# Float16 parts for the input projection's last eight tiles, in a one-core encoder layer

## The chip, the cores and the metric

The kernel runs on one core of a Trainium2 chip. The metric is the device time of one launch in microseconds; lower is better. A core has five engines that work beside each other, each in its own listed order: TensorE (PE, matmuls; PEld is its weight load), VectorE (DVE), ScalarE (ACT), GpSimd (POOL) and SyncE (SP), on whose queue most DMA transfers are issued.

## The reference

One encoder layer on 1024 tokens of width 1024: a normed input, one projection to 2304 columns, two token mixers on its parts, an output projection, and a gated MLP with a depthwise convolution.

```python
hn = rmsnorm(h, norm_mix[l])
proj = jnp.einsum('bsd,de->bse', hn, w_in[l])
qa, ka, va, qb, kb, vb = jnp.split(proj, splits, axis=-1)
...
o_a = window_gqa_sink(qa, ka, va, sink[l])                # |i-j| <= 128, 8 heads
o_b = neighbourhood_attention(qb, kb, vb, rpb[l])         # 8 x 16 window on a 16 x 64 grid, 8 heads
mix = jnp.concatenate([rmsnorm(o_a, norm_a[l]), rmsnorm(o_b, norm_b[l])], axis=-1)
h = h + jnp.einsum('bse,ed->bsd', mix, w_out[l])
hn = rmsnorm(h, norm_ffn[l])
h = h + conv_gated_mlp(hn, w_gate[l], w_up[l], conv_w[l], conv_b[l], w_down[l])
return rmsnorm(h, norm_final)
```

All values are float32.

## The kernel before

Activations lie transposed, with features on the 128 partitions and tokens along the free axis. A float32 product is made of three matmuls on a high and a low part of each operand: high by high, high by low, low by high. `block` issues these three for one 128 by 128 weight block and 512 tokens (half `h` of the 1024). In the input projection the parts are of the type float32r (rows of the profile call it f32); in the output projection (`product16`, L180) and the MLP (L1197 to L1199) they are float16, with scales found on the chip.

The input projection has 18 tiles of 128 columns. `Project(m)` makes tile `m`: 8 blocks (`k`, 128 features each) for each half, 16 blocks or 48 matmuls. Its right operands are `xg[k]`, the high and low part of x times the norm gain, 16 tiles of 512 KB under the tag "xg". Its weights come in two loads (`load`, `load_rest`), each of 4 blocks: `fetch_w` loads a raw tile, `halve_w` (L156, L157) makes `whi` on ScalarE and `wlo` on VectorE or, from unit 12 of the attention on, on POOL. `evacuate` (L269, L273) multiplies the result by `rstd1`, the row factors of the norm, and `post` turns it into attention operands.

Tiles 0 to 2 are made ahead. The others, then the first half of the output projection (`OutA`), form a list `jobs` that is run by a generator, `rest`, as filler between the attention's steps: the loop over `units` (16 units of the window, 32 of the grid) issues scores, transposes and value products, and calls `fill` after each, at the rates in `RATES`. That fixes TensorE's order by hand. The other engines' order comes from a scheduler, which follows the order of writing, priorities and its own estimates. The dictionary `aux` holds extra steps by (number of the job, number of its block); the job of tile `m` has the number `m - 3`.

A score row goes through VectorE (L466, with the mask or bias), ScalarE (exponential, L470), VectorE (reciprocal, L471), and then reaches the value product by one of several paths: scaled on POOL (L474) and transposed on TensorE (L498), then split by ScalarE and VectorE (L501, L502); or split first (L480, L481, L484 to L491) and transposed by a DMA on SP's queue ("flip", L492). `split_v` (L353 on) scales and splits values with ScalarE (L375) and VectorE (L376).

Before the attention, `scan_out` loads the 8 tiles of the output weights once and sums their squares on ScalarE (L761); from these `out_scales`, an `aux` step at (8, 3), finds the scale `wo_by` of the output weights' float16 parts, with two transposes on TensorE (L255).

Of the kernel before, what the change touches and what calls it, by code (L numbers as in the profile page):

```python
# [13 lines left out]
F32 = mybir.dt.float32  # L14
# [42 lines left out]
V_TOP, P_TOP, TINY = 2.0 ** 14, 2.0 ** 15, 1e-30  # L57
X_TOP, W_TOP, FAINT = 2.0 ** 7, 2.0 ** 13, 1e-24
W_ROOT = W_TOP * 2.0 ** 63

K_ID, K_MA, K_MB, K_SCALE, K_END = 0, 128, 512, 896, 897


def hybrid_layer(tc, xT, w_in, w_out, w_gate, w_up, w_down, small, sink, rpb, consts, rope, out):
    nc = tc.nc
    with ExitStack() as ctx:
# [92 lines left out]

        def load_w(src):  # L160
            return halve_w(fetch_w(src))

        def load_w16(src):

# [188 lines left out]
        def split_v(t, rows):  # L353

            n = rows.stop - rows.start
            top, down = (vpool.tile([128, 1], F32, name=x, tag=x) for x in ("top", "down"))
            up = cpool.tile([128, 1], F32, name="up", tag="up", bufs=6)
            nc.vector.tensor_reduce(top[rows], t[rows, :], axis=mybir.AxisListType.X, op=ALU.max, apply_absolute_value=True)
            nc.vector.tensor_scalar(top[rows], top[rows], TINY, None, op0=ALU.max)
# [267 lines left out]
        class Project:  # L627
            def __init__(self, m):
                self.m, self.grid = m, m >= 6

            def load(self):
                raw, self.raw = (fetch_w(w_in[self.m, :, k:k + 4, :]) for k in (0, 4))
                self.w = halve_w(raw)

            def load_rest(self):
                self.w += halve_w(self.raw)

            def run(self):
                self.t = tmp("t")
                if self.m < 17:  # L640
                    for h in range(2):
                        ps = bank("pj", "pj")
                        yield from product(ps, self.w, xg, h)
                        with tc.high_priority(offset=500), behind(*["low"] * (self.m == 3 and h == 1)):
                            evacuate(self.t, ps, h, self.grid)
                else:

                    ps = [bank("pj", "pj") for _ in range(2)]
                    for h, k in [(h, i - 3 * h) for i in range(KT + 3) for h in range(2) if 0 <= i - 3 * h < KT]:
                        block(ps[h], self.w[k], xg[k], h, k == 0, k == KT - 1)  # L650
# [104 lines left out]
        wo_rows = cpool.tile([128, KT], F32, name="wo_rows")  # L755
        mix_up, wo_by, wo_back = (cpool.tile([128, 1], F32, name=x) for x in ("mix_up", "wo_by", "wo_back"))

        def scan_out(d):
            t = big("scan", "op")
            nc.sync.dma_start(t, w_out[d].rearrange("p k c -> p (k c)"))  # L760
            nc.scalar.activation(t, t, AF.Square, accum_out=wo_rows[:, d:d + 1])  # L761
# [68 lines left out]
        def rest():  # L830
            for i, job in enumerate(jobs[1:]):
# [3 lines left out]
                for n, _ in enumerate(job.run()):  # L835
                    yield True
                    if i == 0:
                        if n == 8:
                            with behind("copied"):
                                for p in first:  # L840
                                    make_stacks(p)
                        continue
                    if n == REST and i + 2 < len(jobs):
                        jobs[i + 2].load_rest()
                    settle(n)
                    if (i, n) in aux:
                        aux[i, n]()
# [38 lines left out]
        aux[11, 8] = square_a  # L886
        for h in range(2):
            aux[12, 10 + 3 * h], aux[13, 1 + 2 * h] = (lambda h=h: narrow_a(h)), (lambda h=h: wide_a(h))
        for i in range(4):
            aux[13, 3 * i + 4], aux[13, 3 * i + 6] = normed_a(i, 0), normed_a(i, 1)  # L890
        def out_scales():

            m = top(par[:, C_NA:C_NA + 8], "pt", "og")
# [14 lines left out]
        SCAN_OUT_AT, OUT_SCALES_AT = [], (8, 3)  # L908
        for d, x in enumerate(SCAN_OUT_AT):
            aux[x] = lambda d=d: scan_out(d)  # L910
        aux[OUT_SCALES_AT] = out_scales
        aux[13, 3] = lambda: (wide_a(1), gains_up(0))
        filler = rest()
        live["op"] = 2 + sum(needs(m) for m in range(3))

# [993 lines left out]
```

## Time and profile before

| | |
|---|---|
| median of 3 runs | 1028.36 us (1027.37 to 1029.76) |
| profiled execution | 1028.71 us, span 1026.6 us |
| busy over the span | PE 1009.0, PEld 577.2, DVE 875.2, ACT 675.8, POOL 214.6 us |
| granted clock of TensorE | 0.997 |
| input projection with attention | to about 301 us |
| output projection | to about 410 us |

A row of a group gives the line, the engine, the operation, output and inputs, their shape and type, the count, then busy time and the mean of one in ns, then the idle time before it and what ended it. In rows in order of time the first two numbers are start and duration in us.

### The profile page before, as it was taken

To read this page: it belongs to the slowest core of one execution; us is meant where nothing else is said; L and a number is where in the kernel's file an instruction comes from. 1 tells how busy PE (TensorE), PEld (TensorE's weight loads), DVE (VectorE), ACT (ScalarE), POOL (GpSimd) and SP (SyncE) were. 2 spreads that over 40 slices of the span, in tenths; PEclk is the share of its full clock that TensorE was granted. 3 is DMA by queue.
4 is the path that set the end of the run, shared out by engine and by line. 5 is a ranking of instruction groups with operands and counts; after the bars stand their busy time and mean duration, and the time that the engine had idled before them with its cause. 6 is when DMAs were issued, how large, how long until landed. Compare 5 with 4: busy or idle time off the path is not lost.

```text
span 1026.6 us, 15663 instructions
## 1 busy us (share of the span) xinstructions
PE 1009.0 (98%) x5102; PEld 577.2 (56%) x5102; DVE 875.2 (85%) x1715; ACT 675.8 (66%) x1242; POOL 214.6 (21%) x339
## 2 busy tenths in 40 slices
PE   8999999999999999999999999999999999999996
PEld 6877777777775555544444444444444444444446
DVE  6799997767898799999897989888888879999865
ACT  7667787768687687645777777844544656655551
POOL 2225545777976210001000000000000000000002
PEclk9999999999999999999999999999999999999998
DMA  8566564786799874201787777723232778978734
GB/s 318 194 134 134 111 141 102 154 160 134 141 190 226 287 254 165 82 1 42 258 279 248 262 242 250 246 99 128 87 122 89 256 250 306 309 242 269 257 141 164
DMA packets 143938, 191.79 MB, mean 187 GB/s; under 512 B 77360, under 2 KB 88112, under 8 KB 143856
## 3 DMA queue, kind: packets, MB, share of 16 engines
q1 hardware_dynamic: 133264, 164.84, 56.2%
q10 hardware_dynamic: 10592, 25.95, 6.6%
q8 instruction: 40, 0.66, 0.3%
q14 instruction: 42, 0.34, 0.1%
HBM read 132.81 MB, written 28.57 MB: 157 GB/s over the span
## 4 chain that ended last, share of the span: by engine, by line
PE 75%; DVE 3%; DMA 2%; ACT 1%; issue 0%; POOL 0%; DVEq 0%; ACTq 0%; POOLq 0%
PE pj L180 7%; PE dn L1199 6%; PE dn L1198 6%; PE dn L1197 6%; PE z L1197 5%; PE z L1198 5%; PE z L1199 5%; PE x L1197 4%; PE y L1197 4%; PE x L1198 4%; PE y L1198 4%; PE y L1199 4%; PE x L1199 4%; PE pj L172 3%; PE pj L174 2%; PE pj L173 2%
## 5 line engine op out<-in xcount | busy, mean ns | idle before, releaser
L1199 PEld LDWEIGHTS <-wlo 128*128 128x128 f16 x898 | 87.9, 98 | 101.3
L1197 PEld LDWEIGHTS <-whi 128*128 128x128 f16 x898 | 88.1, 98 | 100.3
L1198 PEld LDWEIGHTS <-whi 128*128 128x128 f16 x898 | 87.9, 98 | 100.2
L1199 PE MATMUL dn<-xd,wlo 128*128 128x512 f16 (+1 forms) x330 | 120.4, 365 | 0.0
L1198 PE MATMUL dn<-xd,whi 128*128 128x512 f16 (+1 forms) x330 | 120.4, 365 | 0.0
L1197 PE MATMUL dn<-xd,whi 128*128 128x512 f16 (+1 forms) x330 | 120.4, 365 | 0.0
L172 PE MATMUL pj<-xgh,whi 128*128 128x512 f32 x248 | 106.8, 431 | 0.0
L1197 PE MATMUL z<-hg,whi 128*128 128x512 f16 x264 | 100.1, 379 | 0.0
L1198 PE MATMUL z<-hg,whi 128*128 128x512 f16 x264 | 100.1, 379 | 0.0
L1199 PE MATMUL z<-hg,wlo 128*128 128x512 f16 x264 | 100.1, 379 | 0.0
L470 ACT ACTIVATE p<-p,nm 128x385 f32<-128x385 f32 (+3 forms) x128 | 74.8, 584 | 35.7 <-DVE nm L466 27.1
L174 PE MATMUL pj<-xgh,wlo 128*128 128x512 f32 x248 | 97.7, 394 | 0.0
L173 PE MATMUL pj<-xgl,whi 128*128 128x512 f32 x248 | 97.4, 393 | 0.0
L1171 ACT ACTIVATE whi<-ws,m 128x512 f16<-128x512 f32 (+1 forms) x96 | 65.9, 708 | 35.6 <-DVE ws L1338 20.4
L1172 DVE SCALAR_TENSOR_TENSOR wlo<-ws,m,whi 128x512 f16<-128x512 f32 (+1 forms) x96 | 70.2, 741 | 17.9 <-ACT whi L1171 17.7
L1052 POOL TENSOR_TENSOR back<-back,cst 128x4 f32<-128x4 f32 (+1 forms) x7 | 2.8, 394 | 356.7 <-DVE back L1051 356.7
L1186 ACT ACTIVATE scan<-scan 128x1024 f32<-128x1024 f32 (+1 forms) x60 | 61.1, 1018 | 18.0 <-DMA scan<-in_w_down_dram 13.6
L1171 ACT ACTIVATE whi<-raw,m 128x512 f16<-128x512 f32 (+1 forms) x78 | 51.3, 699 | 17.7 <-DMA raw<-in_w_down_dram 9.6
L1172 DVE SCALAR_TENSOR_TENSOR wlo<-raw,m,whi 128x512 f16<-128x512 f32 (+1 forms) x78 | 55.4, 731 | 6.9 <-ACT whi L1171 6.9
L1197 PE MATMUL y<-hg,whi 128*128 128x512 f16 x160 | 60.6, 379 | 0.0
L1198 PE MATMUL y<-hg,whi 128*128 128x512 f16 x160 | 60.6, 379 | 0.0
L1199 PE MATMUL y<-hg,wlo 128*128 128x512 f16 x160 | 60.6, 379 | 0.0
(299 smaller groups left out, 2457.7 us busy)
## 6 DMA issues: line engine op xcount, KB each, us to landing
xd<-x SPq DMA_DIRECT2D x77, 256.0 KB, 5.5
raw<-in_w_down_dram SPq DMA_DIRECT2D x64, 256.0 KB, 3.6
x<-c ACTq DMA_DIRECT2D x22, 512.0 KB, 3.7
scan<-in_w_gate_dram SPq DMA_DIRECT2D x18, 512.0 KB, 4.5
scan<-in_w_up_dram SPq DMA_DIRECT2D x18, 512.0 KB, 6.1
raw<-in_w_gate_dram SPq DMA_DIRECT2D x18, 512.0 KB, 3.9
raw<-in_w_up_dram SPq DMA_DIRECT2D x18, 512.0 KB, 3.5
raw<-in_w_in_dram SPq DMA_DIRECT2D x32, 256.0 KB, 3.1
```

Of the source, the lines that this page charges most:

```text
L172: nc.tensor.matmul(ps, w[0], x[0][:, tsl(h)], start=first, stop=False)
L173: nc.tensor.matmul(ps, w[0], x[1][:, tsl(h)], start=False, stop=False)
L174: nc.tensor.matmul(ps, w[1], x[0][:, tsl(h)], start=False, stop=last)
L180: nc.tensor.matmul(ps, a, b, start=i == 0 and b is x[h][0] and a is w[0], stop=i == len(ws) - 1 and a is w[1])
L470: nc.scalar.activation(p[:, 0:e], p[:, 0:e], AF.Exp, bias=nm, scale=-1.0, accum_out=sm)
L1052: nc.gpsimd.tensor_tensor(back, back, unit_back.to_broadcast([128, n]), op=ALU.mult)
L1171: mark["whi"] = nc.scalar.activation(hi, src, AF.Copy, scale=by)
L1172: nc.vector.scalar_tensor_tensor(lo, src, by, hi, op0=ALU.mult, op1=ALU.subtract)
L1186: nc.scalar.activation(t, t, AF.Square, accum_out=dst)
L1197: nc.tensor.matmul(ps, w[0], x[0], start=first and i == 0, stop=False, skip_group_check=True)
L1198: nc.tensor.matmul(ps, w[0], x[1], start=False, stop=False, skip_group_check=True)
L1199: nc.tensor.matmul(ps, w[1], x[0], start=False, stop=last and i == len(ws) - 1, skip_group_check=True)
```

## The change

Tiles 10 to 17 of the input projection take float16 parts instead of float32r: tiles 10 and 11 for the blocks k = 0 to 3 (their blocks k = 4 to 7 stay float32r, with weights scaled alike), tiles 12 to 17 for all. For this

- `scan_in` takes the place of `scan_out` at the start: it loads the weight tiles 10 to 17 and sums their squares on ScalarE;
- `in_tops` and `in_scales`, during tile 8, find scales for x and the weights from the gains, the smallest row factor and these sums: three reductions and some column operations on VectorE, two transposes on TensorE, three operations on POOL;
- `x_fetch` loads the 8 tiles of x a second time, four during tile 9 and four during tile 11, into places of the tag "xg"; `x_halve` makes the float16 parts from them, the high one on ScalarE, the low one on VectorE;
- `halve_w16` and `halve_scaled` first scale the raw weights in place on ScalarE, then split them on ScalarE and POOL;
- `rstd1` is multiplied on ScalarE, at the start of tile 10, by the inverse of the scales;
- tiles 9 to 12 are made in another order, four blocks for each half, then the other four for each half, tiles 10 and 11 with k = 4 to 7 first, in two banks of PSUM at a time;
- the scans of the output weights (`fetch_out`, `scan_out`) are spread over tiles 12 to 14, and `out_scales` moves to tile 15.

```diff
+G_MIN, Y_TOP = 2.0 ** -40, 2.0 ** 9
+HALF_AT = (10, 12)
+M_END = 18
...
+        def halve_w16(raw):
+            hi, lo = (wpool.tile([128, 4, 128], F16, name=n, tag=n, padded_shape=[128, 8, 128]) for n in ("whi", "wlo"))
+            nc.scalar.activation(raw, raw, AF.Copy, scale=wi_by)
+            nc.scalar.activation(hi, raw, AF.Copy)
+            nc.gpsimd.tensor_tensor(lo, raw, hi, op=ALU.subtract)
...
+            def halve(self, i, raw):
+                how = halve_w if self.m < HALF_AT[0] else halve_w16 if self.m >= HALF_AT[i] else halve_scaled
...
+                self.turned = HALF_AT[0] <= self.m < HALF_AT[1]
+                order = (1, 0) if self.turned else (0, 1)
...
+                x = [x16[k] if self.m >= HALF_AT[k // 4] else xg[k] for k in range(KT)]
+                if HALF_AT[0] - 1 <= self.m <= HALF_AT[1]:
+                    ps = [bank("pj", "pj") for _ in range(2)]
+                    for i in (1, 0) if self.turned else (0, 1):
+                        for h in range(2):
+                            for k in range(4 * i, 4 * i + 4):
+                                block(ps[h], self.w[k], x[k], h, k % 4 == 0 and (i == 1) == self.turned, k % 4 == 3 and (i == 0) == self.turned)
+                                yield
...
+        def fetch_out(d):
+            wo_scan[d] = big("scan", "xg")
+            nc.sync.dma_start(wo_scan[d], w_out[d].rearrange("p k c -> p (k c)"))
         def scan_out(d):
-            t = big("scan", "op")
-            nc.sync.dma_start(t, w_out[d].rearrange("p k c -> p (k c)"))
+            t = wo_scan.pop(d)
             nc.scalar.activation(t, t, AF.Square, accum_out=wo_rows[:, d:d + 1])
...
+        def in_tops():
+            for i, rows in enumerate((par[:, C_NMIX:C_NMIX + 8], wi_rows)):
+                nc.vector.tensor_reduce(wi_top[:, i:i + 1], rows, axis=mybir.AxisListType.X, op=ALU.max, apply_absolute_value=True)
+            nc.vector.tensor_reduce(x_least, rstd1, axis=mybir.AxisListType.X, op=ALU.min)
...
+        def x_fetch(k):
+            x_again[k] = big("xt", "xg")
+            nc.sync.dma_start(x_again[k], xT[k])
+        def x_halve(k):
+            t = big("x16", "xg").bitcast(F16)
+            hi, lo = x16[k] = t[:, 0:S], t[:, S:2 * S]
+            by = x_gains[:, k:k + 1]
+            nc.scalar.activation(hi, x_again[k], AF.Copy, scale=by)
+            nc.vector.scalar_tensor_tensor(lo, x_again[k], by, hi, op0=ALU.mult, op1=ALU.subtract)
...
-        for d in range(KT):
-            scan_out(d)
+        for m in range(HALF_AT[0], M_END):
+            scan_in(m)
...
+        at(HALF_AT[0] - 5, 3, in_tops)
+        at(HALF_AT[0] - 5, 8, in_scales)
+        at(HALF_AT[0] - 3, 1, lambda: nc.scalar.activation(rstd1, rstd1, AF.Copy, scale=wi_back))
+        for i, m in enumerate((HALF_AT[0] - 1, HALF_AT[1] - 1)):
+            for k in range(4):
+                at(m - 3, 5 + k, lambda k=4 * i + k: x_fetch(k))
+                at(m - 3, 8 + 2 * k, lambda k=4 * i + k: x_halve(k))
...
-        aux[OUT_SCALES_AT] = out_scales
+        for d in range(KT):
+            at(9 + d // 3, 2 + 5 * (d % 3), lambda d=d: fetch_out(d))
+            at(9 + (d + 1) // 3, (7, 12, 2)[d % 3], lambda d=d: scan_out(d))
+        at(12, 6, out_scales)
```

Lines in the rows below are those of each program: L191 to L193 of the new one are L172 to L174 of the old (`block`), L456 is L436 (scores), L490 is L470 (exponential), L512 is L492 (flip).

TensorE at the 79th score row, before:

```order
1209 L172 MATMUL pj<-xgh,whi 128x512
1210 L173 MATMUL pj<-xgl,whi 128x512
1211 L174 MATMUL pj<-xgh,wlo 128x512
1212 L436 MATMUL s<-ka,q 128x384
1213 L436 MATMUL s<-kb,q 128x384
```

and the same place now, where `x_2719` is the pair of float16 parts of x's tile k = 4:

```order
1280 L191 LDWEIGHTS whi
1281 L191 MATMUL pj<-x_2719,whi 128x512
1282 L192 LDWEIGHTS whi
1283 L192 MATMUL pj<-x_2719,whi 128x512
1284 L193 LDWEIGHTS wlo
1285 L193 MATMUL pj<-x_2719,wlo 128x512
1286 L456 MATMUL s<-ka,q 128x384
1287 L456 MATMUL s<-kb,q 128x384
```

The number and order of the matmuls is the same; the float16 ones have a weight load listed apart, and use float16 tiles.

ScalarE during tile 9, from the 47th exponential of the attention on, before:

```order
184 L470 ACTIVATE p,sm<-p,nm 128x385
185 L501 ACTIVATE turned<-pt 128x3x128
186 L485 ACTIVATE stage<-p,by 128x3x128
187 L470 ACTIVATE p,sm<-p,nm 128x385
188 L480 ACTIVATE hl<-p 128x3x128
189 L501 ACTIVATE turned<-pt 128x3x128
190 L470 ACTIVATE p,sm<-p,nm 128x385 x2
```

and now, with L851 for the high half of one tile of x (`x_2149` and so on) from the reloaded `xt`, and L170 for a half of the weights:

```order
191 L505 ACTIVATE stage<-p,by 128x3x128
192 L851 ACTIVATE x_2149<-xt,cells 128x1024
193 L490 ACTIVATE p,sm<-p,nm 128x385
194 L170 ACTIVATE whi<-raw 128x512
195 L490 ACTIVATE p,sm<-p,nm 128x385
196 L521 ACTIVATE turned<-pt 128x3x128
197 L851 ACTIVATE x_2172<-xt,cells 128x1024
198 L500 ACTIVATE hl<-p 128x3x128
199 L490 ACTIVATE p,sm<-p,nm 128x385
200 L556 ACTIVATE ot<-o 64x256
201 L851 ACTIVATE x_2225<-xt,cells 128x1024
202 L851 ACTIVATE x_2256<-xt,cells 128x1024
```

Four halvings, each behind a load of 512 KB, have come between the exponentials.

SP's queue at that place, before:

```order
78 L492 DMA_TRANSPOSE turned<-stage 128x6x128
79 L150 DMA raw<-in_w_in_dram 128x512
80 L492 DMA_TRANSPOSE turned<-hl 128x6x128
81 L492 DMA_TRANSPOSE turned<-stage 128x6x128 x2
82 L492 DMA_TRANSPOSE turned<-hl 128x6x128
83 L150 DMA raw<-in_w_in_dram 128x512
```

and now, with L844 for `x_fetch`:

```order
81 L512 DMA_TRANSPOSE turned<-stage 128x6x128
82 L844 DMA xt<-in_xT_dram 128x1024 x3
83 L512 DMA_TRANSPOSE turned<-stage 128x6x128
84 L844 DMA xt<-in_xT_dram 128x1024
85 L153 DMA raw<-in_w_in_dram 128x512
86 L512 DMA_TRANSPOSE turned<-hl 128x6x128
87 L844 DMA xt<-in_xT_dram 128x1024 x3
88 L512 DMA_TRANSPOSE turned<-stage 128x6x128 x2
```

Seven of the eight loads of x now stand within seven rows, between the flips, and behind one another.

More of the change, by code (lines that the diff above doesn't have):

```diff
@@ L161, in load_w, with halve_scaled @@
             return halve_w(fetch_w(src))
+        def halve_w16(raw):
[3 more added lines that the diff above has]
+            nc.gpsimd.tensor_tensor(lo, raw, hi, op=ALU.subtract)
+            return [(hi[:, j, :], lo[:, j, :]) for j in range(4)]
+        def halve_scaled(raw):
+            hi, lo = (wpool.tile([128, 4, 128], F32R, name=n, tag=n) for n in ("whi", "wlo"))
+            nc.scalar.activation(raw, raw, AF.Copy, scale=wx_by)
+            nc.scalar.activation(hi, raw, AF.Copy)
+            nc.gpsimd.tensor_tensor(lo, raw, f32(hi[:, :, :]), op=ALU.subtract)
+            return [(hi[:, j, :], lo[:, j, :]) for j in range(4)]
         def load_w16(src):
@@ L355, in split_v @@
             n = rows.stop - rows.start
-            top, down = (vpool.tile([128, 1], F32, name=x, tag=x) for x in ("top", "down"))
+            topdown = vpool.tile([128, 2], F32, name="top", tag="top")
+            top, down = topdown[:, 0:1], topdown[:, 1:2]
             up = cpool.tile([128, 1], F32, name="up", tag="up", bufs=6)
@@ L845, in rest @@
                     settle(n)
-                    if (i, n) in aux:
-                        aux[i, n]()
+                    for f in aux.get((i, n), ()):
+                        f()
                 if i == 0:
```

60 lines of the change are left out of this document (46 added, 14 removed).

## The prediction

> **What bounds the kernel now.** I read the page's shares and chain first, then the groups by line, the stretches of the attention, the waits of TensorE, and last single matmuls in order of time.
>
> ```profile
> PE 1009.0 (98%) x5102; PEld 577.2 (56%) x5102; DVE 875.2 (85%) x1715; ACT 675.8 (66%) x1242; POOL 214.6 (21%) x339
> PE 75%; DVE 3%; DMA 2%; ACT 1%; issue 0%; POOL 0%; DVEq 0%; ACTq 0%; POOLq 0%
> ...
> L172 PE MATMUL pj<-xgh,whi 128*128 128x512 f32 x248 | 106.8, 431 | 0.0
> L1197 PE MATMUL z<-hg,whi 128*128 128x512 f16 x264 | 100.1, 379 | 0.0
> ```
>
> TensorE (PE) is busy for 98% of the span and carries the chain of waits. The durations in a matmul's row include its way through the array, so 431 and 379 ns are no prices: what one costs is the step from its start to the next start. The change concerns projection tiles 10 to 17, and those fall between about 170 and 301 us (the evacuations of L273, two a tile from tile 6 on, run from 98.5 to 301.2 us). How full are the engines there, and does TensorE ever stop?
>
> ```profile
> 130.00:150.00 20.00, 19.04 (x107) 14.31 (x106) 17.87 (x54) 16.16 (x42) 10.29 (x23) 1.00 0.76 156
> 150.00:170.00 20.00, 20.00 (x117) 15.32 (x115) 15.92 (x50) 15.09 (x39) 9.67 (x21) 1.00 0.33 73
> 170.00:190.00 20.00, 19.56 (x116) 14.94 (x115) 16.73 (x60) 15.86 (x43) 12.11 (x20) 1.00 0.68 137
> 190.00:205.00 15.00, 14.79 (x82) 11.38 (x81) 9.50 (x38) 9.54 (x25) 12.91 (x18) 1.00 0.82 173
> 205.00:255.00 50.00, 50.00 (x275) 39.22 (x274) 34.66 (x103) 35.85 (x80) 36.72 (x44) 1.00 0.76 148
> 255.00:301.00 46.00, 46.00 (x260) 36.18 (x259) 40.91 (x106) 34.18 (x73) 38.81 (x43) 1.00 0.83 158
> ...
> L273 DVE TENSOR_TENSOR t<-pj,rstd x24: 669/682/692, 98.5 to 301.2; 128x512 f32<-128x512 f32 x24
> ...
> PE o L525 <- DVE by L484: 1.4, 1, 1.4
> PE pt L498 <- POOL p L474: 1.4, 3, 0.7
> PE pj L180 <- DVE mg L1144: 1.2, 1, 1.2
> ```
>
> The columns of the stretches are length, then PE, PEld, DVE, ACT, POOL busy, the granted clock (1.00 throughout) and DMA share. From 150 to 301 us TensorE is busy 150.35 of 151 us while no other engine is full. The three waits shown are its longest from 60 to 420 us and sum to 4.0 us. So in the stretch of the change its own instructions set the time, and what shortens them shortens the span, as long as nothing else fills up.
>
> **The change, part by part. 1. Cheaper matmuls.** A block is three matmuls of 512 columns. Tiles 10 and 11 move 8 of their 16 blocks to float16, tiles 12 to 17 all 16: 112 blocks, 336 matmuls. Float32 blocks with nothing between, and float32 and float16 blocks amid attention, stand in order of time:
>
> ```profile
> 21.83 0.39 PE L172 MATMUL o<-xgh,whi 128*128 128x512 f32 x1
> ...
> 23.89 0.39 PE L172 MATMUL pj<-xgh,whi 128*128 128x512 f32 x1
> ...
> 201.07 0.40 PE L172 MATMUL pj<-xgh,whi 128*128 128x512 f32 x1
> ...
> 203.21 0.40 PE L172 MATMUL pj<-xgh,whi 128*128 128x512 f32 x1
> ...
> 203.92 0.50 PE L601 MATMUL o<-turned,v 128*128 128x128 f16 x4
> ...
> 310.23 0.60 PE L180 MATMUL pj<-mg,whi 128*128 128x512 f16 x2
> ...
> 310.88 0.49 PE L601 MATMUL o<-turned,v 128*128 128x256 f16 x4
> ...
> 312.22 0.60 PE L180 MATMUL pj<-mg,whi 128*128 128x512 f16 x2
> ```
>
> Nine float32 matmuls from 21.83 to 23.89 are 0.229 us each, 0.687 a block. Amid attention one block, 203.21 to 203.92, is 0.71; a float16 one, 310.23 to 310.88, is 0.65. The whole pattern of block, four value matmuls, block, two scores takes 2.14 us (201.07 to 203.21) in float32 and 1.99 (310.23 to 312.22) in float16: 0.075 a block. So the ends are 112 x (0.687 - 0.65) = 4.1 us and 112 x 0.075 = 8.4; I take the single-block rows, nearest in kind and place, 112 x 0.06 = **6.7 us less**. Float16 matmuls have a separate weight load in the instruction list where float32 ones have none, but the trace's float16 blocks have that too, so 0.65 includes it.
>
> The Trainium skill speaks against this gain: "TensorE: Matmul & The Clock Gate", section "Back-to-back issue gap", gives one warm gap, N/2.4 + 2.5 ns, with no word of the type, so 216 ns for 512 columns in either. By it this term would be 0, and the sum below would be 3.4 us slower instead of 3.3 faster. The trace has 0.217 for float16 (0.65 by three) but 0.229 to 0.237 for float32, so the formula holds for the one and not for the other.
>
> **2. ScalarE (ACT).** Added work, by the nearest rows:
>
> ```profile
> L375 ACT ACTIVATE vhl<-t,down 128x1024 f16<-128x1024 f32 x4 | 4.5, 1136 | 0.0
> L167 ACT ACTIVATE whi<-raw,wo_by 128x512 f16<-128x512 f32 x8 | 5.7, 711 | 0.9 <-PE pj L180 0.9
> L761 ACT ACTIVATE scan<-scan 128x1024 f32<-128x1024 f32 x8 | 8.4, 1056 | 0.0
> L761 ACT ACTIVATION_READ_ACCUMULATOR scan<-scan 128x1 f32 x8 | 1.6, 196 | 0.0
> ...
> 26.97 1.05 ACT L761 ACTIVATE scan<-scan 128x1024 f32<-128x1024 f32 x1
> ...
> 28.00 1.06 ACT L761 ACTIVATE scan<-scan 128x1024 f32<-128x1024 f32 x1
> ```
>
> Eight high halves of x at 1.14 us are 9.1; sixteen scalings of half a weight tile in place at 0.71 are 11.4; eight out-weight scans, formerly before the attention, at 1.25 are 10.0 (the input-weight scans take their old place one for one, at no cost); the scaling of the row factors 1.1. That is 31.6 us. By place: 150 to 190 us gets four halves of x, four scalings and the row factors, 8.5, on 30.95 of 40; 190 to 205 four halves and two scalings, 6.0, on 9.54 of 15; 205 to 255 the scans and six scalings, 14.3, on 35.85 of 50. So ScalarE's busy time comes to 39.5 of 40, 15.5 of 15 and 50.2 of 50. Busy time overstates it: a scan's two rows sum to 1.25, but the next scan starts 1.03 after it (26.97 to 28.00), so about 0.1 us an instruction overlaps. With 187 instructions there before and 37 more, up to 22 of the 105 us are overlap, though part of it shows as no busy time already; I put real use near 90 to 95%. What does such a load do to TensorE? Slices of before that are as full:
>
> ```profile
> 240.00:250.00 10.00, 10.00 (x58) 7.87 (x57) 6.27 (x19) 8.29 (x19) 5.57 (x9) 1.00 0.76 161
> 290.00:300.00 10.00, 10.00 (x58) 7.86 (x58) 9.29 (x22) 9.15 (x17) 7.25 (x7) 1.00 0.93 190
> 300.00:310.00 10.00, 9.35 (x57) 5.80 (x56) 9.01 (x29) 8.88 (x21) 6.88 (x9) 1.00 1.18 250
> 360.00:370.00 10.00, 8.82 (x43) 4.16 (x42) 10.00 (x21) 9.74 (x19) 0.00 (x0) 1.00 0.75 294
> ...
> 360.00:410.00 50.00, 48.82 (x265) 26.89 (x264) 47.26 (x85) 39.73 (x70) 4.27 (x7) 1.00 0.60 210
> ```
>
> With ACT at 8 to 9 tenths TensorE lost nothing or 0.65; at 9.74 beside a full DVE it lost 1.18. Ends for 105 us: 0, since nothing is taken from ScalarE that could give a gain, and 10.5 x 1.18 less the 0.65 that TensorE idles there already (19.56 of 20, 14.79 of 15), some 11.7. I take 2.5, a quarter of a microsecond a slice, near the fuller slices of the attention itself (0 and 0.65), since scores run ahead of the values that use them.
>
> **3. VectorE (DVE), POOL, TensorE's new steps.** Eight low halves of x at 1.31 (row below) are 10.5 us: 5.2 in 150 to 170, on 15.92 of 20, so over it in busy time and carried into 170 to 190; 5.2 in 190 to 205, where 5.5 are free. The reduction over the row factors (1.21) lands early, after the first tiles' evacuations near 46 us, where VectorE works without a break. I price what of both shows on TensorE at 0.6, between 0 and 1.21 + 1.2 (one carry as large as the excess of 21.1 over 20). POOL keeps its subtractions and gains a few column operations of 0.25 to 0.6 us: no cost, since the scores' scaling waits for VectorE there. Two transposes (0.27 each) and the scan's move past OUT_SCALES add 0.3 on TensorE.
>
> ```profile
> L376 DVE SCALAR_TENSOR_TENSOR vhl<-t,down,vhl 128x1024 f16<-128x1024 f32 x4 | 5.2, 1310 | 0.0
> L358 DVE TENSOR_REDUCE top<-t 128x1 f32<-128x1024 f32 x4 | 4.8, 1210 | 0.0
> ...
> xt<-in_xT_dram SPq DMA_DIRECT2D x6, 512.0 KB, 6.1
> xr<-in_xT_dram SPq DMA_DIRECT2D x6, 512.0 KB, 4.6
> scan<-in_w_out_dram SPq DMA_DIRECT2D x8, 512.0 KB, 8.4
> q1 hardware_dynamic: 133264, 164.84, 56.2%
> ```
>
> **4. Transfers.** Sixteen loads of 512 KB move into 150 to 255 us on SP's queue, among the flips (DMA transposes of the probabilities). The main queue's 164.84 MB took 56.2% of the span, 577 us, so 8.4 MB take 29 of 105 us and raise a DMA share of 0.33 to 0.82 by 0.28. Alone that is hidden, as 205 to 255 us ran at 0.76 with TensorE at 50.00. Their latency is not free: the first x loads wait until TensorE has used the float32 tiles they overwrite, and ScalarE's four halvings stand within four exponentials of each other (its order, in the section on the change). That is in the 2.5 above, and beyond it a rival.
>
> Sum: -6.7 + 2.5 + 0.6 + 0.3 = **-3.3 us**. The profiled execution took 1028.71 us (span 1026.6), 0.35 above the median of 1028.36; from the latter, **1025.1 us**.
>
> **The rivals.** (a) The covers hold: 2 and 3 cost nothing but the transposes, 1028.4 - 6.7 + 0.3 = 1022.0. For it: scores run ahead by two or three units, and the waits of 4.0 us in 360. Against: the sums at 15.5 of 15. (b) ScalarE and VectorE fill up and pace the attention: 5 to 6 us given back, about 1028. For it: the same sums, and VectorE at 40.91 of 46 behind. (c) Slower: ScalarE held by loads. It works in its listed order; if an x tile or a scan lands late, every exponential behind it waits, then POOL's scaling, then the transposes, which already wait thrice for POOL above. A load in a queue took 8.4 us where 4.6 is the free time, so up to 3.8 late; a set of four x tiles holds that once, and two sets and two bursts of scans make 4 x 3.8 = 15 on ScalarE, of which it decides when more than 6.7 - 3.4 = 3.3 reach TensorE. With half through, 1028.4 - 3.3 + 7 = 1032. (d) No gain by type: 1028.4 + 3.4 = 1031.8; for it only that 0.229 lies near 0.217, against it the float16 pattern at 1.99. It is what the Trainium skill's gap formula, above, would give.
>
> **How the numbers follow.** Forecast 0.43 (own range 1023.4 to 1026.2); (a) 0.17; (b) 0.25; (c) 0.12; (d) 0.03. A measurement here tells 0.2%, 2.06 us, from no change. Faster: 0.43 + 0.17 = 0.60; same: (b) 0.25; slower: 0.15. The range leaves out (c), (d) and the outer part of (a), and reaches through (b): 1021.7 to 1029.6.
>
> **What would show it.** Right: float16 blocks of pj at 0.65 us a block; the last evacuation of tile 17 some 3 us before 301.2; the FFN stages as long as before; ScalarE above 90% from 150 to 255 us, with TensorE's busy time there short by 2 to 4 us. Wrong: blocks still at 0.70; waits of ScalarE for xt or scan over a microsecond each, with pt or o waiting behind (c); or TensorE without gaps (a). A gain that appears by 301 us and is gone by 410 would mean that the next stage was paced by VectorE (47.26 of 50 in 360 to 410), which I leave at nothing since its work follows TensorE's results.

## The result, and the profile after

The changed kernel took 1054.2 us (median of 6 runs, 1052.07 to 1058.1) against 1028.72 for the kernel before (6 runs): a ratio of 1.0253, 95% interval 1.0238 to 1.0269. It is 25.5 us slower; 3.3 us faster had been forecast. The profiled execution has a span of 1050.7 us (1026.6 before). Two executions further below ran at a granted clock of 0.65 (1497 and 1499 us) and are left out of the ratios, and since the only profile of the kernel with the high half first is of one of them, its waits are not read. The lines that answer to those shown of before, from the page, the stretches, the evacuations and TensorE's waits from 60 to 440 us:

```profile
PE 1012.7 (96%) x5104; PEld 555.0 (53%) x5104; DVE 886.9 (84%) x1734; ACT 702.6 (67%) x1283; POOL 220.5 (21%) x343
PE 62%; DVE 4%; DMA 3%; ACT 2%; issue 1%; SPq 0%; POOL 0%; DVEq 0%; ACTq 0%; POOLq 0%
```

```profile
130.00:150.00 20.00, 19.05 (x107) 14.25 (x106) 17.03 (x58) 15.82 (x40) 11.58 (x25) 1.00 0.67 148
150.00:170.00 20.00, 18.45 (x103) 13.48 (x101) 17.64 (x46) 17.97 (x39) 10.98 (x20) 1.00 0.63 173
170.00:190.00 20.00, 16.01 (x85) 10.82 (x83) 16.43 (x53) 16.09 (x40) 10.96 (x17) 0.91 0.86 225
190.00:205.00 15.00, 14.98 (x85) 10.39 (x84) 12.36 (x35) 12.76 (x30) 12.02 (x14) 1.00 0.59 99
205.00:255.00 50.00, 44.51 (x253) 25.50 (x251) 29.70 (x91) 40.37 (x89) 31.10 (x40) 1.00 1.01 224
255.00:301.00 46.00, 40.57 (x226) 23.58 (x225) 33.96 (x101) 33.96 (x72) 34.68 (x42) 0.96 0.54 126
```

```profile
L292 DVE TENSOR_TENSOR t<-pj,rstd x24: 671/680/692, 97.9 to 322.0; 128x512 f32<-128x512 f32 x24
```

```profile
PE pt L518 <- POOL p L494: 7.7, 7, 3.6
PE o L621 <- ACT turned L521: 3.8, 4, 1.5
PE o L621 <- DVE mixb L637: 2.4, 1, 2.4
```

From 150 to 301 us TensorE is now busy 134.5 of 151 us (150.35 before), and the last evacuation comes at 322.0 instead of 301.2. Yet no engine is full there: ScalarE has 87.2 of 105 us in 150 to 255. So the time was lost in waits, and the list of waits names their last releaser, first of all the softmax's POOL step, not their cause. ScalarE's own waits, 140 to 350 us, say more:

```profile
ACT raw L169 <- DMA raw<-in_w_in_dram: 10.6, 5, 4.0
ACT p L490 <- DVE nm L486: 9.8, 12, 1.6
ACT whi L186 <- DMA raw<-in_w_out_dram: 3.6, 2, 3.3
```

Before the change the longest were these (same stretch); no load of input weights is in that whole list:

```profile
ACT p L470 <- DVE nm L466: 21.4, 28, 2.3
ACT stage L485 <- DVE by L484: 7.1, 11, 1.2
ACT whi L156 <- PE pj L173: 3.8, 4, 1.6
```

So ScalarE, which had waited for results to work on, now waits for weights as well. One such wait, first the last step of a row maximum (`nm`) on VectorE, then ScalarE's instructions in order of time, and then TensorE's waits just behind them:

```profile
214.17 0.08 DVE L486 DVE_READ_ACCUMULATOR2_ANT nm<- 128x1 f32 x1
...
213.52 0.62 ACT L170 ACTIVATE whi<-raw 128x512 f16<-128x512 f32 x1
218.09 0.72 ACT L169 ACTIVATE raw<-raw,cells 128x512 f32<-128x512 f32 x1 [3.95 <-DMA raw<-in_w_in_dram]
218.72 0.70 ACT L347 ACTIVATE ka<-t,cst 128x512 fp32r<-128x512 f32 x1
219.33 0.60 ACT L490 ACTIVATE p<-p,nm 128x384 f32<-128x384 f32 x1
...
220.33 0.38 PE L621 MATMUL o<-turned,v 128*128 128x256 f16 x2 [0.84 <-DVE sm L491]
225.48 0.22 PE L621 MATMUL o<-turned,v 128*128 128x128 f16 x1 [1.35 <-ACT turned L521]
```

ScalarE stands idle for 3.95 us until the weights for the in-place scaling (L169) land. The exponential (L490) that needs this `nm` could have had it at 214.25, and starts only behind the scaling, at 219.33. The Trainium skill, "PSUM — Partial Sum Buffer", section "Engine vs sequencer instructions", calls the queues of ScalarE, VectorE and GpSimd strict FIFO; the trace agrees, as nothing was run in the 3.95 us although that exponential's operand was there.

### The profile page after: what moved, and what is told of

It reads as the page before. It is cut to its first block, busy times and chain, and to the rows that moved or that the text cites. A ratio compares the mean times of both kernels' runs of the same rounds, so it can differ in the third digit from the quotient of the medians.

```text
span 1050.7 us, 15744 instructions
## 1 busy us (share of the span) xinstructions
PE 1012.7 (96%) x5104; PEld 555.0 (53%) x5104; DVE 886.9 (84%) x1734; ACT 702.6 (67%) x1283; POOL 220.5 (21%) x343
## 4 chain that ended last, share of the span: by engine, by line
PE 62%; DVE 4%; DMA 3%; ACT 2%; issue 1%; SPq 0%; POOL 0%; DVEq 0%; ACTq 0%; POOLq 0%
PE pj L199 6%; PE dn L1302 6%; PE dn L1300 6%; PE dn L1301 6%; PE z L1300 5%; PE z L1301 5%; PE z L1302 5%; PE x L1300 3%; PE y L1300 3%; PE x L1301 3%; PE y L1301 3%; PE y L1302 3%; PE x L1302 3%; DMA raw<-in_w_down_dram 1%; DMA raw<-in_w_out_dram 1%
## 5 line engine op out<-in xcount | busy, mean ns | idle before, releaser
L490 ACT ACTIVATE p<-p,nm 128x385 f32<-128x385 f32 (+3 forms) x128 | 74.5, 582 | 26.8 <-DVE nm L486 22.2
L456 PE MATMUL s<-ka,q 128*128 128x384 f32 (+1 forms) x128 | 56.0, 438 | 3.0 <-DVE turned L522 2.3
L1705 DVE SCALAR_TENSOR_TENSOR xd<-xd,m 128x512 f16<-128x512 f32 x77 | 55.1, 747 | 3.9 <-ACT xd L1704 3.9
L191 PE MATMUL pj<-xgh,whi 128*128 128x512 f32 x136 | 58.1, 427 | 0.0
```

The costliest lines, as they stand in the source:

```text
L191: nc.tensor.matmul(ps, w[0], x[0][:, tsl(h)], start=first, stop=False)
L456: nc.tensor.matmul(ps[:, 0:n], qs, k[i][:, cs[0] * 128:cs[0] * 128 + n], start=i == 0, stop=i == 1)
L490: nc.scalar.activation(p[:, 0:e], p[:, 0:e], AF.Exp, bias=nm, scale=-1.0, accum_out=sm)
L1705: nc.vector.scalar_tensor_tensor(lo, t[:, HALF:S], by, hi, op0=ALU.mult, op1=ALU.subtract)
```

## The experiments

Terms of the expectations: H, ScalarE is held by the place of the scaling; S, the sheer work on ScalarE; O, the late scans of the output weights; X, the second x; P, TensorE's new order; Q, a faster TensorE outruns the others; T, a threshold of the sum (in the run with the high half first in the whole kernel: x and the scans take the gain); L, a late load of output weights; A, the parts add; M, two holds overlap. Differences between kernels below are differences of ratios times 1028.4 us, good to some 2 us. "Row r" is score row r, counted from 0 (the matmuls of L456 or its line in each kernel). This table gives how much longer than in the kernel before it took from row 12 to row r, from the starts of those matmuls in each trace:

```
row                     56     64     76     84     92     96    108    116    124
start in before, us  163.8  179.2  207.1  228.4  249.6  260.1  293.1  311.7  327.9
changed kernel        +1.8   +7.0   +7.0   +9.6  +12.5  +17.2  +19.6  +19.8  +25.4
e5 bare               +1.4   +1.2   -0.1   -1.4   -2.7   -2.2   -2.9   -2.9   +3.5
e7 bare, scaling      +1.5   +2.9   +4.8   +3.5   +7.2  +12.0  +14.4  +14.3  +20.9
f2 bare, hi first     +1.2   +0.6   +0.2   -1.0   -2.3   +0.5   +0.3   +1.8   +6.8
f7 bare, x            +1.4   +7.5   +6.2   +5.0   +3.7   +4.2   +3.5   +3.4  +10.4
f6 bare, out first    +1.0   +0.8   -0.5   -1.8   -3.0   -2.6   -3.2   -3.3   -0.3
g1 no scaling         +1.3   +5.8   +4.5   +6.4   +9.9  +13.4  +12.6  +12.7  +20.9
g2 scans ahead        +2.6   +7.2   +5.6   +4.3   +3.1   +7.5   +7.3   +9.0  +14.0
```

**One part away at a time.** First run: the scaling moved to POOL.

```diff
-            nc.scalar.activation(raw, raw, AF.Copy, scale=wi_by)
-            nc.scalar.activation(hi, raw, AF.Copy)
+            nc.scalar.activation(hi, raw, AF.Copy, scale=wi_by)
+            nc.gpsimd.tensor_scalar(raw, raw, wi_by, 1.0, op0=ALU.mult, op1=ALU.mult)
             nc.gpsimd.tensor_tensor(lo, raw, hi, op=ALU.subtract)
```

> The changed kernel, but ScalarE scales no weights in place: it makes the high half straight from the raw tile with the scale (one instruction, as before the change), and POOL scales the raw tile and subtracts. 16 ScalarE instructions of 0.71 us go (11.4 us) and 16 go to POOL. To be explained are 25.5 us (1054.2 against 1028.7) and the 6 to 7 us that the float16 matmuls gain, some 32 in all. Theory H (ScalarE held: the scaling, whose only cover is the load, stands in its order before the exponentials and waits for late loads, 10.6 us in five waits): the held time goes as well as the work, so 15 us or more are gained, 1039 or less. Theory S (sheer work: 31.6 us were added to ScalarE, each costs TensorE about as much): 11.4 of them go, 1043. Theory O (the out-weight scans in tiles 12 to 14) or theory X (the second load and halving of x) as the main cause: 1050 or more.

1053.69 us, ratio 1.0245 (1.023 to 1.026): 0.8 us less than the changed kernel. Second, without the scans (the loop over `fetch_out` and `scan_out` replaced by `nc.gpsimd.memset(wo_rows, 1.0)`):

> The changed kernel without the eight loads and scans of the output weights (left out: their sums of squares are set to 1, so the scale is that of other weights). 4 MB and 10.0 us of ScalarE go from tiles 12 to 14 (about 205 to 255 us). Theory O: most of the loss after 200 us goes, 12 us or more, 1042 or less, and tiles 12 to 17 lose no more on TensorE than tile 10 and 11. Theory S: 10 of 31.6, 1044. Theory H: the raw loads of tiles 13 to 15 come earlier without the scans' on their queue, but the scalings still wait: 1046 to 1050. Theory X: 1051 or more.

1052.76 us, 1.0241 (1.0225 to 1.0257). Third, `x_fetch` empty and `x_halve` a `memset` of the float16 tile:

> The changed kernel without the second load of x and without its halving on ScalarE and VectorE (left out: the float16 parts of x are filled with a constant by POOL). 4 MB, 9.1 us of ScalarE and 10.5 of VectorE go from 150 to 205 us. Theory X: 12 us or more are gained, 1042 or less, above all in tiles 9 to 12 (last evacuations of tile 11 some 8 us earlier). Theory S: 9.1 of 31.6, 1045. Theory H or O: 1048 or more.

1052.66 us, 1.0235 (1.022 to 1.025). Fourth, all three:

> All three together: weights scaled on POOL, no scans of the output weights, no second x (left out: as in the two runs above). What is left of the change is the float16 matmuls, the scan of the input weights in place of the other, the scales, the row factors' scaling and the new order of tiles 9 to 12. If the added ScalarE work and its waits are the cause, whichever of H, S, O, X has the larger part, 1022 to 1024, the before less the gain of the matmuls. Rival P (the new order of TensorE's blocks, two banks at a time, or the scales' chain costs TensorE itself): 1030 or more.

1040.18 us, 1.0115 (1.0098 to 1.0132). No single part is worth 2 us from above, all together are worth 14, and 1022 is far off. Taken together, these runs would dismiss every one of H, S, O and X as the main cause, wrongly as the next ones show. The fourth run probably also suffers from its replacement: POOL's fills are 1.8 us each, POOL is in the path of the softmax, and TensorE waits 9.1 us for POOL's scaling there (7.7 in the changed kernel).

```profile
L850 POOL MEMSET x<- 128x2048 f16 x8 | 14.4, 1811 | 0.0
```

**From the bottom up.** So the parts were taken away without work in their place, and put back singly. For the bare kernel `x16[k]` is a view of `xg[k]`'s memory, the scans are away, and

```diff
-            nc.scalar.activation(raw, raw, AF.Copy, scale=wi_by)
-            nc.scalar.activation(hi, raw, AF.Copy)
+            nc.scalar.activation(hi, raw, AF.Copy, scale=wi_by)
```

> The float16 matmuls with as little around them as can be. Left out: the scans of the output weights (sums set to 1), the scaling of the raw weights in place (the high half takes the scale in its one instruction, the low half is subtracted from the unscaled raw tile, as many instructions as before the change), and the second x: the float16 operands are views of the float32 tiles' own memory, so no engine and no transfer fills them. What is left is the float16 matmuls, the scales' chain in tile 8, the row factors' scaling and the new order of tiles 9 to 12. In the fourth run POOL had 14.4 us of fills and 10.6 us of scalings instead, and its slices at 140 to 180 us lost 4.9 of 40 us on TensorE. Theory S/H (added ScalarE work and its waits are all): 1022 to 1024. Theory P (two-bank order of tiles 9 to 12): 1028 to 1036, with the loss in 140 to 240 us. Theory Q (TensorE, being faster, outruns VectorE, ScalarE and POOL, so that the matmuls' gain turns into waits): 1026 to 1030, with short waits spread over 200 to 300 us.

> As the run before (the same parts left out), and tiles 9 to 12 in the old order, eight blocks of one half and then eight of the other, one bank of PSUM at a time, weights k = 0 to 3 first. The same number of matmuls of each type. Theory P: 4 us or more below the run before, near 1022. Theories S/H and Q: within 1.5 us of it.

Bare: 1031.17 us, 1.0027 (1.0015 to 1.0038). In the old order: 1030.8, 1.0021 (1.0011 to 1.003). P falls: the old order is 0.6 us faster, which is within the noise. But the floor of the change lies 2.8 us above the kernel before, not 6 below it. The table shows why: the bare kernel gains 4.1 us from row 64 to row 116, as the cheaper matmuls should, and then loses 6.4 by row 124. Q is a part of it: in the stretch of the gain TensorE's waits grew from 0.9 to 2.7 us. The next two put parts back: the scaling as the change has it, and the scans alone.

> The bare kernel with the 16 in-place scalings of raw weights put back, as the change has them (out-weight scans and second x still left out). Theory H: 6 us or more above the bare kernel, with ScalarE waiting for weight loads as in the changed kernel. Theory S: 11.4 / 31.6 of the loss between the bare and the changed kernel, about a third of it. Theory T (no part alone costs much; TensorE loses only when ScalarE's sum passes a threshold, as taking away one part alone gained 1 to 2 us): less than 3 us.

> The bare kernel with the eight out-weight loads and scans put back in tiles 12 to 14 as the change has them (scaling in place and second x still left out). Theory O: 6 us or more above the bare kernel, between 205 and 260 us. Theory S: about a third of the loss between the bare and the changed kernel. Theory T: less than 3 us.

The scaling: 1048.05 us, 1.0188 (1.0171 to 1.0205), 16.6 above bare for 11.4 us of work. The scans: 1033.42, 1.0048 (1.0033 to 1.0063), 2.2 above bare. ScalarE's waits in the run with the scaling, then the load, the scaling and the high half of one weight tile there, and the load and the high half of the same tile in the bare kernel (L169 is the high half there; the row with x2 holds two high halves, the second is this tile's):

```profile
ACT raw L169 <- DMA raw<-in_w_in_dram: 20.1, 10, 3.2
```

```profile
232.21 0.53 SPq L153 DMA_DIRECT2D raw<-in_w_in_dram  x1
235.47 0.72 ACT L169 ACTIVATE raw<-raw,cells 128x512 f32<-128x512 f32 x1 [2.54 <-DMA raw<-in_w_in_dram]
245.04 1.14 ACT L170 ACTIVATE whi<-raw 128x512 f16<-128x512 f32 x2
```

```profile
224.16 0.53 SPq L153 DMA_DIRECT2D raw<-in_w_in_dram  x1
236.24 0.72 ACT L169 ACTIVATE whi<-raw,cells 128x512 f16<-128x512 f32 x1 [1.03 <-PE pj L190]
```

The high half needs the place of old weights, and starts 12 us after its load was issued; a load that lands late within that time costs nothing. The scaling needs nothing but the load, so it stands at the landing, 3.3 us after the issue, some 10 us sooner than anyone needs it. To separate place from work, two instructions are exchanged:

```diff
-            nc.scalar.activation(raw, raw, AF.Copy, scale=wi_by)
-            nc.scalar.activation(hi, raw, AF.Copy)
+            nc.scalar.activation(hi, raw, AF.Copy, scale=wi_by)
+            nc.scalar.activation(raw, raw, AF.Copy, scale=wi_by)
```

In ScalarE's order the scaling of one tile (`raw_3188`) and its high half, first ahead, then behind:

```
301 L169 ACTIVATE raw_3188<-raw_3188,cells_333 128x512
314 L170 ACTIVATE whi_3192<-raw_3188 128x512
---
310 L169 ACTIVATE whi_3192<-raw_3188,cells_333 128x512
312 L170 ACTIVATE raw_3188<-raw_3188,cells_333 128x512
```

> The bare kernel (no out-weight scans, float16 x as views: left out as there) with the 16 scalings on ScalarE, but after the high half. The bare kernel took 1031.2, with the scalings ahead of the high half 1048.0. Theory H: 1036 or less. Theory S: 1046 or more, since the work is the same.

1035.54 us, 1.0067 (1.0051 to 1.0083). Of the 16.6 us, 12.4 were the place and 4.1 the work. No wait for input weights is left in ScalarE's list (20.1 us with the scaling ahead). In the two traces some other instructions have changed places too, as the scheduler orders anew, and no run keeps that apart; the same exchange on the kernel before, further below, gives the same sign. In the whole changed kernel:

> The whole changed kernel with two ScalarE instructions of each split exchanged: the high half is made first, straight from the raw tile with the scale, and the raw tile is scaled in place after it. The same 32 instructions of the same sizes, the same transfers; but the scaling now waits for the high half, which itself waits for the place of the old weights, and so it leaves the place directly behind the load: there it stood 2 to 24 places ahead of the high half in ScalarE's order (16 before the scaled rows of one tile), and in the run with the scalings alone ScalarE waited 20.1 us for weight loads at it, which the bare kernel never did. Theory H (the place, not the work): 8 us or more below the changed kernel, 1046 or less, ScalarE's waits for input weight loads gone. Theory S (the work): within 2 us of 1054. Theory T (x and the scans hold ScalarE so that this gain is lost to them, as for the run with the scaling on POOL): 1050 to 1054 although those waits are gone.

1052.95 us, 1.0243 (1.0226 to 1.0261): 1 us, within the noise, as T had it; that the waits for weights are gone there no usable trace shows. So something else fills in. The second x on the bare kernel:

> The bare kernel with the second load of x and its halving on ScalarE and VectorE put back as the change has them (scans and scaling in place left out). Theory X: 6 us or more above the bare kernel's 1031.2, between score rows 52 and 72 (155 to 195 us). Theory S: 9.1 of 31.6 of the 23 us between the bare and the changed kernel, 6 to 7, spread. Theory T: less than 3.

1036.9 us, 1.0083 (1.0066 to 1.0099), 5.8 above bare, and against that kernel the table puts 6.3 between rows 56 and 64. There VectorE's low half of x (its 1.61 us) stands ahead of a reciprocal, on which POOL's scaling and then TensorE wait:

```profile
175.30 1.61 DVE L850 SCALAR_TENSOR_TENSOR x<-xt,cells,x 128x1024 f16<-128x1024 f32 x1
177.02 0.16 DVE L489 RECIPROCAL sm<-sm 128x1 f32<-128x1 f32 x1
177.56 0.55 PE L516 MATMUL pt<-cst,p 128*128 128x128 f32 x3 [2.96 <-POOL p L492]
```

And the loss from row 116 to 124 that all these kernels have:

```diff
-            raw = fetch_w(src)
+            with tc.high_priority(offset=200):
+                raw = fetch_w(src)
```

> The bare kernel with the eight loads of the first half of the output weights given an earlier place on SP's queue (a priority of 200 at the load alone; nothing else is edited; the fifth and sixth load go from places 200 and 203 of the queue to 191 and 199, as 191 and 204 before the change). All kernels with the change lose 3 to 7 us at one place, between score rows 121 and 122 (at 322 us in the profile of before), where ScalarE waits 2.7 to 3.2 us for such a load, an exponential stands behind it, and TensorE waits for POOL 3.0 to 3.4 us with a lower granted clock after it. Theory L (that load's place on the queue): 4 to 6 us below the bare kernel, 1025 to 1027, which is below the kernel before. Rival (VectorE or POOL paces that place, the wait of ScalarE only shows it): within 1.5 us of 1031.

1027.36 us, 0.9989 (0.998 to 0.9999), 3.9 below bare: L holds. In the bare kernel the output projection's high half waits for its load, and TensorE stops behind it:

```profile
322.03 0.72 ACT L184 ACTIVATE whi<-raw,wo_by 128x512 f16<-128x512 f32 x1 [3.17 <-DMA raw<-in_w_out_dram]
...
327.04 0.90 PE L516 MATMUL pt<-cst,p 128*128 128x128 f32 x3 [3.42 <-POOL p L492]
```

Its load was issued at 317.76; the fifth load, which it is, in the kernel before at 305.00 and in this run at 303.15, with no wait over 1.6 us left on TensorE. Why the change moved that load on SP's queue was not settled.

**The whole kernel.** What takes the gain back when the scaling is mended?

> The whole changed kernel with the 16 in-place scalings left out (the low half is subtracted from the unscaled tile); second x and out-weight scans stay where the change has them. From the bare kernel upward the parts cost 16.8 (scalings ahead), 5.7 (x) and 2.3 us (scans), together 24.8, near the 23 that the changed kernel lies above it; from the changed kernel downward taking one away gives 1.5. In the bare kernel with scans alone, though, their loads ran at 158 to 171 us, since no x tiles held the places of the tag that they share, and not at 214 to 249 as in the changed kernel. Theory A (the parts add): 1031.2 + 5.7 + 2.3 = 1039. Theory M (two holds overlap: where ScalarE no longer waits for a weight tile it waits for a scan's transfer a little later, so the late scans are worth some 12 us once the scaling is mended, which is what the run with the high half first left unexplained): 1047 to 1050, with waits of ScalarE for scans of 4 us or more.

1050.16 us, 1.0219 (1.0202 to 1.0236): M, at the upper end, and not A. With x in place the scans run at 217 to 250 us instead of 162 to 191 and cost 14.0 us (against the bare kernel with x), where the bare kernel without x had 2.2. With the scaling present, in the second run, the same scans cost 1.2. ScalarE's waits without the scaling:

```profile
ACT p L488 <- DVE nm L484: 13.3, 19, 1.6
ACT scan L803 <- DMA scan<-in_w_out_dram: 6.9, 5, 3.1
ACT whi L184 <- DMA raw<-in_w_out_dram: 4.7, 2, 3.4
```

Two holds of one engine in one stretch overlap: whoever waits for the weights finds the scan landed, and the other way round. The changed kernel has no wait for a scan in its list and 10.6 us of waits for weights; in the second run, without scans, those for weights are longer:

```profile
ACT raw L169 <- DMA raw<-in_w_in_dram: 17.4, 10, 3.2
```

Then the scans were put ahead of the attention, behind `scan_in`, in three kernels that compute everything.

> The changed kernel with the high half first, and the out-weight scans ahead of the attention, behind those of the input weights (as before the change, where they alone stood there; out_scales stays in tile 15). Nothing is left out. Theory M: 1031.2 (bare) + 5.7 (x) + 4.3 (the scalings behind the high half) = 1041, up to 1044 if eight more scans ahead of the attention show. Rival (the scans' place is not what takes the gain back): 1050 or more.

> The run before, and the out-weight loads of the output projection's first half with priority 200. Nothing is left out. By theory L, 3.8 us below the run before: 1037 to 1040. If the place of that load matters only in the bare kernel: no change.

> The run before with no scaling on ScalarE at all: the low half is made by VectorE in one instruction from the raw tile, the scale and the high half (as the output projection does, 0.74 us each in the rows there), and POOL has none of it. Nothing is left out. 11.4 us less on ScalarE, 17.8 less on POOL, some 10.4 more on VectorE. If only ScalarE counts: 4.3 below the run before, about 1034; if VectorE paces where it is full: the same or above. In no case below the kernel before, by the sum of the bare kernel with the load mended (1027.4) and x (5.7), 1033.

1059.23 us (1.0309, 1.0285 to 1.0332), 1058.36 (1.0292, 1.0276 to 1.0307) and 1055.44 (1.0264, 1.0248 to 1.0279): all above what was expected, by 15 us and more. The scans hold ScalarE ahead of the attention too; its wait, and TensorE's for weights that ScalarE then halves late, in the first of them up to 140 us:

```profile
ACT scan L805 <- DMA scan<-in_w_out_dram: 9.7, 4, 6.2
...
PE pj L191 <- ACT whi L159: 10.0, 1, 10.0
```

Up to row 12 it lost 18.3 us. From there on its budget closes: 14.0 by row 124, against 3.5 (bare) + 6.9 (x) + 3.3 (scaling behind) = 13.7 from the table. The earlier output load gained nothing by row 124 there (13.9 by the same reckoning), so L holds for the bare kernel alone.

**On the kernel before.** Last, the scaling alone, with float32r tiles, first ahead and then behind the high half:

```diff
+            if scaled:
+                nc.scalar.activation(raw, raw, AF.Copy, scale=unit)
             mark["weights"] = nc.scalar.activation(hi, raw, AF.Copy)
...
-                self.w = halve_w(raw)
+                self.w = halve_w(raw, self.m >= 10)
```

> The kernel before, nothing of the change in it but one thing: the raw weights of tiles 10 to 17 are scaled in place on ScalarE (by 1.0, so that the values stay) ahead of their high half, 16 instructions of about 0.71 us. Two one-column tiles share one to make room, as in the change. Theory H (the scaling leaves the place behind the old weights and stands at the load's landing): 10 us or more slower, 1038 to 1046, with ScalarE waiting for weight loads, which it never did there. Theory S (the work): 4 to 6 us. If the hold needs the float16 matmuls: less than 2.

> As the run before, with the high half first and the scaling behind it: the same instructions, two of them exchanged. Theory H: 3 to 5 us slower than the kernel before (it was 4.3 on the bare kernel). Theory S: as the run before.

1041.76 us, 1.0134 (1.0119 to 1.0149), and 1034.78, 1.0061 (1.0044 to 1.0078). So sixteen copies on an engine that is two thirds busy cost 13.8 us ahead and 6.3 behind: 7.5 for the place; the 6.3 lie above the 3 to 5 that H allowed, by less than the noise. The first has the wait again, and the second has none for weights in its list:

```profile
ACT raw L160 <- DMA raw<-in_w_in_dram: 16.8, 12, 3.1
```

No run points to a version that beats both kernels: the best, at 0.9989, leaves x, scans and scaling out.

## Why the prediction was wrong, point by point

**The matmuls were right, their reach was not.** The pattern of block, four value matmuls, block, two scores takes 1.99 us, as forecast (first rows of two patterns and the first block's end):

```profile
308.80 0.39 PE L191 MATMUL pj<-x,whi 128*128 128x512 f16 x1
...
309.46 0.49 PE L621 MATMUL o<-turned,v 128*128 128x128 f16 x4
...
310.79 0.39 PE L191 MATMUL pj<-x,whi 128*128 128x512 f16 x1
```

A block is 0.66 us, so rival (d) is out. Of the 6.7 us some 6.0 are in the steps of the best bare kernel (the one with the earlier output load): from row 64 to row 116, where all 112 blocks lie, it takes 4.1 us less than the kernel before, with TensorE's waits up by 1.9. But 3.0 of the 4.1 are gone by row 124, where TensorE, come earlier, waits for flips (TensorE's waits in that kernel, 60 to 440 us):

```profile
PE o L620 <- DMA turned<-hl: 1.6, 1, 1.6
...
PE o L620 <- DMA turned<-stage: 1.2, 1, 1.2
```

So even that kernel ends no more than 1.1 us ahead. With x, scans and scaling away the prediction's terms leave 6.4 us of gain (rival (a), 1022.0); the bare kernel lost 2.8, so some 9 us of the miss lie here and not in the added work.

**The step that failed is the second term, 2.5 us for ScalarE.** With VectorE's 0.6 it priced at 3.1 us what lies between the bare and the changed kernel, measured 23.2: some 20 us of the miss. Its sum of work was about right (busy time rose by 26.8 us). The failure is that 31.6 us were priced by the fullness of ten-microsecond slices, as if an instruction could wait for a free moment. The row used for the scaling, L167 at 711 ns with 0.9 us of idle time, belongs to an instruction that waits for TensorE to leave the old weights, long after its load; the new one has no such wait in front of it and stands at the load's landing. Measured on the bare kernel it is 16.6 us, of which 12.4 are place. The scans are the second such case, 14.0 us where the scaling is away.

**Rival (c) had the mechanism and not the instruction.** It saw an in-order ScalarE held by loads, exponentials behind, then POOL, then the transposes: the chain of the trace. But it counted four bursts of x and scans, 15 us on ScalarE and half of it through, and gave it 0.12. The sixteen scalings, each behind a load, were not on its list, though the diff shows them with nothing but the load to wait for. Rival (b), full engines, is not what happened: ScalarE has 83% in 150 to 255 us.

**The small terms.** VectorE's 0.6 was too little: x cost 5.8 with ScalarE's part, most of it in one stretch. The two transposes, put at 0.3, take 0.13 us of TensorE's steps in the bare kernel; but all bare kernels are 1.0 to 1.5 us behind by row 56, ahead of any float16 matmul, in the bare kernel 0.5 of it in waits, and the rest is not assigned. That transfers are hidden at a DMA share near 0.8 was wrong for the waiting instruction: three weight loads made ScalarE wait in 205 to 255 us, where the share is 1.01. The share is not needed for it: on the kernel before with the scaling ahead, ScalarE waits there for six, at a share of 0.70. The MLP is as long as before, as forecast: 24.9 us late at row 124, 24.1 at the end.

## What to carry to other kernels

On an in-order engine ask of each added instruction what it waits for last, before asking how long it is: one that waits only for a transfer sits at the landing and holds all that is behind it, and one line's exchange, work after the instruction that was waiting anyway, took 12.4 of 16.6 us away in the bare kernel here. Where several holds share an engine, taking one away can show nothing, so build up from a bare version as well, and replace a removed part by nothing, not by work on another engine.

## What the hardware showed beside that

After stops of 2.3 us and more TensorE's granted clock fell for some 3.4 us, three times in the changed kernel and not once in the first 1000 us before, where the longest wait was 1.4. The slices, and one case (steps of 0.43 us a matmul behind the stop, 0.22 later; between the first row and the second lies another wait, of 0.49 us):

```profile
180.00:190.00 10.00, 7.68 (x38) 5.02 (x36) 7.05 (x27) 6.61 (x17) 4.74 (x7) 0.83 0.73 200
270.00:280.00 10.00, 9.46 (x47) 5.23 (x46) 6.87 (x28) 7.01 (x16) 7.82 (x10) 0.83 0.71 158
340.00:350.00 10.00, 6.43 (x32) 3.95 (x31) 5.93 (x20) 6.23 (x15) 3.23 (x6) 0.83 0.92 281
```

```profile
269.82 0.38 PE L621 MATMUL o<-turned,v 128*128 128x256 f16 x2 [2.40 <-DVE mixb L637]
...
272.62 0.63 PE L192 MATMUL pj<-x,whi 128*128 128x512 f16 x1
273.05 0.63 PE L193 MATMUL pj<-x,wlo 128*128 128x512 f16 x1
...
275.58 0.38 PE L192 MATMUL pj<-x,whi 128*128 128x512 f16 x1
275.80 0.38 PE L193 MATMUL pj<-x,wlo 128*128 128x512 f16 x1
```

The Trainium skill, "TensorE: Matmul & The Clock Gate", section "HAM oscillation — how this bites in real kernels", asks for no idle gaps over some 3.4 us; here falls came behind waits of 2.3, 2.4 and 3.6 us, so its limit is too generous for this kernel. The length of a stop alone does not decide it: in the bare kernel with the scaling ahead the clock fell behind a wait of 1.92 us, and in the bare kernel in the old order it stayed at 1.00 behind one of 2.99. Half speed for 3.4 us (a mean of 0.83 over ten) costs about 1.7 us, so by this estimate the three falls make some 5 of the 25.5 us. The two waits that the rule of length does not fit, in the order named:

```profile
196.66 0.39 PE L621 MATMUL o<-turned,v 128*128 128x256 f16 x2 [1.92 <-DVE mixa L560]
```

```profile
325.01 0.55 PE L516 MATMUL pt<-cst,p 128*128 128x128 f32 x3 [2.99 <-POOL p L492]
```
